# Pooling mixer as band matrices on TensorE, last norm's 1/sigma in PSUM, condition rows in the first MLP

## The chip, the cores and the metric

The kernel runs on one core of one Trainium2 chip, with five engines (PE multiplies matrices; DVE, ACT and POOL work on vectors; SP issues the DMAs), SBUF as working memory and PSUM as the place where PE's sums stand. The metric is the device time of one execution in microseconds, as the median over runs. A profiled execution also leaves a trace with a row for each instruction.

## The reference

One step of a four-layer backbone: 128 prompt tokens and 256 sample tokens, 1024 features, F32. Each layer has a mixer and a squared-ReLU MLP, each followed by a layer norm of ALPHA * x + g * out, with shift, scale and gate from a condition vector (one for the prompt, one for the sample). The mixers are an RG-LRU, a short convolution, multi-scale pooling and the RG-LRU again. The change concerns the third, which subtracts each token from the mean of a window around it (2, 4, 8 or 16 tokens, one window for each quarter of the features, clipped at the sequence's ends) and multiplies each quarter by its own 256 x 256 matrix:

```python
def pool_mixer(x, w, scale):
    ...
    for g, win in enumerate(POOL_WINDOWS):
        lo = jnp.clip(t - win // 2, 0, T)
        hi = jnp.clip(t + win - win // 2, 0, T)
        ...
        s = jnp.take(Sg, hi, axis=1) - jnp.take(Sg, lo, axis=1)
        pooled.append(s / cnt[None, :, None])
    d = (jnp.concatenate(pooled, axis=-1) - xf).astype(x.dtype)
    y = jnp.einsum('btgc,gcd->btgd', d.reshape(bsz, T, N_POOL_GROUPS, POOL_GROUP), w)
    return y.reshape(bsz, T, D_MODEL) * scale
```

and then the layer's last steps, `x = layer_norm(ALPHA * x + g1 * out, ...)` and the MLP with its own norm.

## The kernel before

**Tiles.** Activations lie feature-major: X is eight tiles of 128 features x 384 tokens (128 prompt, 256 sample). Weights stream from HBM in tiles of 1 MB ("raw", four buffers, loaded by SP at L1280), each sixteen blocks of 128 x 128. Half a tile at a time is split into a rounded part `whi` (ACT, L1292) and a rest `wlo` (DVE, L1298), three halves ahead of use. A product is three matmuls in the reduced-precision type fp32r, hi x hi, lo x hi and hi x lo (`mm3`, L195; rows L197, L198, L199), each moving 384 tokens through a stationary weight block. Sums over features, and the modulation's matrix-vector products, use matmuls in full F32.

**Order.** The program is a list of items, most of them a half tile of weights with its blocks. `tick` counts blocks, and `defer(n, f)` keeps f for n ticks later, so work of DVE, ACT and POOL is put between PE's blocks by numbers in the code. A scheduler then sets the row of each engine. Each engine works its row in order.

**A layer norm.** `ln_evac` (L553) takes each finished output tile: `resid` (L549) adds it into X on DVE, one instruction for the prompt's columns and one for the sample's. After tile 0, `shift` (L569, L570) makes `ssb`, its mean over features, and L572 subtracts it from every tile to keep sums small (POOL; DVE for some). L584 squares on ACT; POOL adds tiles into `s1t` (L599), and DVE or POOL squares into `s2t`. `ln_tail` (L611) multiplies `s1t`, `s2t` and the last tile by ones (L621 to L624), and then `tail` (L636) makes 1/sigma on DVE: variance (L650), first guess `y0` (ACT, L651), a Newton step (L655 to L657) into `r`; all these are SBUF tiles `tmp`. L641 subtracts the mean from X (in the last norm POOL does six tiles of it, L649), `chunk` (L660) multiplies a tile by `r` (L661), modulates it (L702, L707), and splits it into the hi and lo pieces of `h` (L720, L725) for the next product. While this runs PE has only modulation products (`gemv`, L347) that were parked for it.

**The pooling layer.** `pool_alloc` (on POOL) clears padded buffers. The tail in front, `ln_tail(4, ..., lazy=True)`, only makes `r`; six of its mean subtractions are on POOL. `pool_mix` (L1132) drives the rest from inside the matrix product: ahead of each group's first block, `stage` scales two tiles (L674), modulates them into padded buffers (L707), and `pool_stage` (L1101) makes window sums on DVE by additions or a scan (L1115 to L1121), corrects the edges (L1129), subtracts the token itself (L1130), and splits, hi on ACT (L720) and lo on POOL (L725). The product then moves 392 columns (L197 to L199). Here L590 adds each tile and its square into the statistics at once by F32 matmuls.

**Condition rows.** `setup_rows` (L424) loads two rows of 1024 conditions and makes silu of them by L427 (ACT), L428 and L429 (DVE), 2048 columns each. `mac` (L432) uses them on DVE (L450) for some modulation products, fed by SP's loads `fetch`.

**Ends.** In `tail`, the last norm's tiles go through `final_y` (L796; L801 on ACT) to the output.

## Time and profile before

| what | value |
|---|---|
| median of three runs | 1638.74 us (1637.17 to 1639.63) |
| the profiled execution's own time | 1636.94 us |
| its span, first to last instruction | 1635.2 us |
| mean granted TensorE clock | 0.987 |
| PE busy | 1568.7 us (96%) |
| DVE busy | 1169.3 us (72%) |
| ACT busy | 751.8 us (46%) |
| POOL busy | 400.6 us (24%) |
| HBM read | 285.64 MB, 176 GB/s over the span |

A busy PE is not PE at its peak: matmuls are pipelined, so a matmul recorded as 0.34 us can start 0.17 us behind the one before. A row of a timeline gives start, duration, engine, line and operation, output <- inputs, shape, the number of instructions in the row (x2), and in square brackets how long the engine was idle before it and which instruction released it. A row of groups gives the busy time and the mean in ns, then the idle time before its instructions and who ended it. In the rows of windows the numbers in brackets are instructions, and the last three columns are the granted clock (1.00 is full), the DMA engines' busy share and GB/s. "PEld" is PE's loading of stationary blocks.

### The profile page before, as it was taken

To read this page: it belongs to the slowest core of one execution; us is meant where nothing else is said; L and a number is where in the kernel's file an instruction comes from. 1 tells how busy PE (TensorE), PEld (TensorE's weight loads), DVE (VectorE), ACT (ScalarE), POOL (GpSimd) and SP (SyncE) were. 2 spreads that over 40 slices of the span, in tenths; PEclk is the share of its full clock that TensorE was granted. 3 is DMA by queue.
4 is the path that set the end of the run, shared out by engine and by line. 5 is a ranking of instruction groups with operands and counts; after the bars stand their busy time and mean duration, and the time that the engine had idled before them with its cause. 6 is when DMAs were issued, how large, how long until landed. Compare 5 with 4: busy or idle time off the path is not lost.

```text
span 1635.2 us, 23710 instructions
## 1 busy us (share of the span) xinstructions
PE 1568.7 (96%) x9304; PEld 1496.4 (92%) x9304; DVE 1169.3 (72%) x1791; ACT 751.8 (46%) x1131; POOL 400.6 (24%) x442
## 2 busy tenths in 40 slices
PE   7999899999999999999997899999999989999996
PEld 6778799999999999999995599999988779999995
DVE  4789999964475569985547899975468997434544
ACT  3796553243253346324434553244359946423432
POOL 2113280002320058110045270000441134000043
PEclk9999999999999999999998999999999999999998
DMA  9776457755343545763533256745333444333321
GB/s 356 271 277 240 181 209 254 269 191 186 126 157 128 184 152 183 257 258 129 196 136 129 105 195 253 272 157 203 129 113 107 158 144 152 128 121 115 126 78 39
DMA packets 42304, 288.77 MB, mean 177 GB/s; under 512 B 4816, under 2 KB 6992, under 8 KB 8144
## 3 DMA queue, kind: packets, MB, share of 16 engines
q1 hardware_dynamic: 42192, 287.25, 49.0%
q8 instruction: 73, 1.20, 0.3%
q14 instruction: 39, 0.32, 0.1%
HBM read 285.64 MB, written 1.59 MB: 176 GB/s over the span
## 4 chain that ended last, share of the span: by engine, by line
PE 79%; DVE 12%; ACT 5%; issue 2%; POOL 1%; DMA 1%; SPq 0%; DVEq 0%; POOLq 0%; ACTq 0%
PE acc L199 26%; PE acc L198 26%; PE acc L197 25%; DVE wlo L1298 2%; DVE lru L881 1%; ACT hidf L932 1%; DMA raw<-in_wmod 1%; DVE hidf L960 1%; DVE X L549 1%; DVE X L572 1%; ACT L935 1%; ACT hidf L935 1%; DVE X L661 1%; DVE hidf L949 1%; POOL h L725 1%
## 5 line engine op out<-in xcount | busy, mean ns | idle before, releaser
L1292 ACT ACTIVATE whi<-raw 128x1024 fp32r<-128x1024 f32 x338 | 356.2, 1056 | 420.2 <-PE acc L199 347.9
L1298 DVE TENSOR_TENSOR wlo<-raw,whi 128x1024 fp32r<-128x1024 f32 x338 | 436.3, 1292 | 156.3 <-ACT whi L1292 155.9
L197 PE MATMUL acc<-h,whi 128*128 128x384 f32 (+2 forms) x1488 | 507.3, 341 | 16.0 <-ACT h L720 10.5
L198 PE MATMUL acc<-h,wlo 128*128 128x384 f32 (+2 forms) x1488 | 505.3, 340 | 0.0
L199 PE MATMUL acc<-h,whi 128*128 128x384 f32 (+2 forms) x1488 | 476.8, 340 | 3.2 <-POOL h L725 3.2
L197 PE MATMUL acc<-hid,whi 128*128 128x384 f32 (+1 forms) x1216 | 411.4, 338 | 0.8 <-ACT hid L977 0.8
L199 PE MATMUL acc<-hid,whi 128*128 128x384 f32 (+1 forms) x1216 | 409.3, 337 | 0.9 <-DVE hid L981 0.9
L198 PE MATMUL acc<-hid,wlo 128*128 128x384 f32 (+1 forms) x1216 | 409.0, 336 | 0.0
L197 PEld LDWEIGHTS acc<-h,whi 128*128 128x128 f32 x1488 | 281.3, 189 | 24.7 <-ACT h L720 11.6
L199 PEld LDWEIGHTS acc<-h,whi 128*128 128x128 f32 x1488 | 278.3, 189 | 6.7 <-POOL h L725 5.0
L198 PEld LDWEIGHTS acc<-h,wlo 128*128 128x128 f32 x1488 | 281.1, 189 | 1.6 <-issue 0.5
L197 PEld LDWEIGHTS acc<-hid,whi 128*128 128x128 f32 x1216 | 228.3, 188 | 2.4 <-ACT hid L977 1.5
L199 PEld LDWEIGHTS acc<-hid,whi 128*128 128x128 f32 x1216 | 228.3, 188 | 1.5 <-DVE hid L981 1.5
L198 PEld LDWEIGHTS acc<-hid,wlo 128*128 128x128 f32 x1216 | 228.3, 188 | 0.9
L450 DVE SCALAR_TENSOR_TENSOR mac<-mac,silb 128x1024 f32<-128x1024 f32 x176 | 216.1, 1228 | 1.7
L832 ACT ACTIVATE tmp<-acc,par 128x384 f32<-128x384 f32 x128 | 74.2, 580 | 248.1 <-PE acc L199 248.1
L572 POOL TENSOR_TENSOR X<-X,ssb 128x384 f32<-128x384 f32 x49 | 56.1, 1179 | 488.7 <-ACT ssb L570 488.7
L834 DVE TENSOR_TENSOR tmp<-tmp 128x384 f32<-128x384 f32 x128 | 73.3, 572 | 104.2 <-ACT tmp L832 104.2
L549 DVE SCALAR_TENSOR_TENSOR X<-acc,m,X 128x128 f32<-128x128 f32 (+1 forms) x176 | 64.7, 411 | 113.9 <-PE acc L199 112.0
L779 POOL TENSOR_SCALAR X<-X,ag,xbb 128x128 f32<-128x128 f32 x64 | 126.9, 1997 | 0.4
L416 POOL TENSOR_SCALAR sc<-m 128x16 f32<-128x16 f32 x7 | 6.4, 911 | 270.8 <-DVE m L464 269.4
L835 DVE TENSOR_TENSOR hid<-tmp,hid 128x384 fp32r<-128x384 f32 x128 | 72.3, 565 | 0.3
(192 smaller groups left out, 1207.1 us busy)
## 6 DMA issues: line engine op xcount, KB each, us to landing
raw<-in_w SPq DMA_DIRECT2D x128, 1024.0 KB, 4.9
mac<-in_wmodv SPq DMA_DIRECT2D x44, 1024.0 KB, 5.0
raw<-in_wmodp SPq DMA_DIRECT2D x26, 1024.0 KB, 4.9
park<-in_wmodp SPq DMA_DIRECT2D x18, 1024.0 KB, 8.4
raw<-in_lin SPq DMA_DIRECT2D x16, 1024.0 KB, 5.1
raw<-in_scin SPq DMA_DIRECT2D x12, 1024.0 KB, 4.9
raw<-in_wmod SPq DMA_DIRECT2D x8, 1024.0 KB, 7.8
raw<-in_lout SPq DMA_DIRECT2D x8, 1024.0 KB, 5.0
```

The costliest lines, as they stand in the source:

```text
L197: pe.matmul(ps, lhsT=hi, rhs=xhi, start=first, stop=False)
L198: pe.matmul(ps, lhsT=lo, rhs=xhi, start=False, stop=False)
L199: late = lambda: pe.matmul(ps, lhsT=hi, rhs=xlo, start=False, stop=last)
L450: vec.scalar_tensor_tensor(prod, raw[i % 2][:, D * q : D * q + D], 1.0, silb[:, D * k : D * k + D], op0=ALU.mult, op1=ALU.mult, accum_out= ...
L549: vec.scalar_tensor_tensor(Xt[c][:, o : o + n], ps[:, a:b], col(g, c, k), Xt[c][:, o : o + n], op0=ALU.mult, op1=ALU.add)
L572: (vec if fast and i > 2 else gp).tensor_tensor(Xt[i], Xt[i], ssb, op=ALU.subtract)
L779: gp.tensor_scalar(Xt[c][:, a:b], Xt[c][:, a:b], col(g, c, k), col(xb, c, k), op0=ALU.mult, op1=ALU.add)
L832: act.activation(r, ps[:, :T], AF.Relu, bias=par_t[:, i : i + 1])
L834: vec.tensor_tensor(q, r, r, op=ALU.mult)
L835: vec.tensor_tensor(lo, q, hi.bitcast(F32), op=ALU.subtract)
L1292: act.activation(hi, raws[id(raw)][:, i * 1024 : (i + 1) * 1024], AF.Copy)
L1298: vec.tensor_tensor(lo, raws[id(raw)][:, i * 1024 : (i + 1) * 1024], hi.bitcast(F32), op=ALU.subtract)
```

## The change

**Pooling.** A window mean minus the token itself is linear in the tokens, so it can be multiplied by a matrix over tokens that is zero outside a band along its diagonal. The new `pool_mix` first multiplies by the weights and then by the band. First stage: for each 128-token block t and group g, z = h^T W, with the block of h stationary and 256 columns of weights moving, three matmuls per k as in `mm3`; two groups share a PSUM buffer of 512 columns, and six such buffers arise. Each is split into hi and lo (ACT L237, DVE L238) in buffers of the MLP's `hid`. Second stage, `second`: for each output tile nine matmuls (L1149) with z stationary and pieces of the band moving, 128, 128, 128, 256, 8, 136, 136, 8 and 136 columns (1064 in all). `first` calls it for tile 0 behind the chunk of X5, for tile 1 behind X6, for the rest behind X7. The tail in front, `ln_tail(4)`, is now an ordinary one with eight chunks. In `ln_evac` for this layer the shift of every tile is on DVE (L571, L581), POOL adds s1t, and the squares are kept and summed by F32 matmuls at the statistics.

**The bands.** `band_load` fetches 128 x 1040 of the bands twice through the raw buffers, copies each into a rounded constant (ACT, L1091) and makes the rest of the parts that need it (DVE, L1095). Both stand behind `ln_tail(2)` in the program.

**Last norm.** For idx 8 the tiles `y0` and `r` are taken from PSUM.

**Condition rows.** `setup_rows` is called from the first `mac` with one of its weight buffers as scratch; its three steps are deferred by 6, 10 and 14 ticks and the second fetch by 15.

In ACT's row around ln_tail(2), `acc` is a PSUM buffer, `tmp_4225` and `tmp_4226` the first chunk. Before, its square of X7 (X_103) is followed by the variance's square, by y0 (L651) and the chunks:

```order
L584 ACTIVATE tmp_4097<-X_102 128x384
L584 ACTIVATE tmp_4158<-X_103 128x384
L643 ACTIVATE tmp_4211<-acc_4160 128x384
L651 ACTIVATE tmp_4213<-tmp_4212 128x384
L707 ACTIVATE tmp_4225<-X_96,bb_2962,gg_2961 128x128
```

After, at the same place, with y0 now L653:

```order
L592 ACTIVATE tmp_4098<-X_102 128x384
L1091 ACTIVATE band<-raw_4119 128x1040
L592 ACTIVATE tmp_4159<-X_103 128x384
L645 ACTIVATE tmp_4212<-acc_4161 128x384
L1091 ACTIVATE band<-raw_4200 128x1040
L653 ACTIVATE tmp_4215<-tmp_4213 128x384
L703 ACTIVATE tmp_4226<-X_96,bb_2963,gg_2962 128x128
```

The two copies stand ahead of the square of X7 and ahead of y0; nothing else has moved here.

DVE's row there after the change, where L657 to L659 are the Newton step:

```order
L657 TENSOR_TENSOR tmp_4214<-tmp_4213,tmp_4215 128x384
L1095 TENSOR_TENSOR fine<-raw_4200,band 128x2x128
L658 SCALAR_TENSOR_TENSOR tmp_4214<-tmp_4214,tmp_4215 128x384
L1095 TENSOR_TENSOR fine<-raw_4200,band 128x2x8 x2
L659 SCALAR_TENSOR_TENSOR tmp_4216<-tmp_4214,tmp_4215 128x384
```

The second band's pieces stand between the Newton step's instructions; the first band's stand ahead of X7's residual.

DVE's row in the pooling layer (X_96 is X0 and so on; `hidf` are the padded buffers). Before, behind tile 2's residual:

```order
L572 TENSOR_TENSOR X_99<-X_99,ssb 128x384
L572 TENSOR_TENSOR X_100<-X_100,ssb 128x384
L572 TENSOR_TENSOR X_101<-X_101,ssb 128x384
L1121 SCALAR_TENSOR_TENSOR hidf_7855<-hidf_7854,hidf_7880 128x408
L1121 SCALAR_TENSOR_TENSOR hidf_7856<-hidf_7854,hidf_7884 128x408
L1124 TENSOR_TENSOR hidf_7857<-hidf_7855 128x392
L1124 TENSOR_TENSOR hidf_7858<-hidf_7856 128x392
L549 SCALAR_TENSOR_TENSOR X_99<-acc_8094,g_7976,X_99 128x128
L549 SCALAR_TENSOR_TENSOR X_99<-acc_8094,g_7976,X_99 128x256
```

After, from the fourth z split on:

```order
L556 SCALAR_TENSOR_TENSOR X_97<-acc_8115,g_8003,X_97 128x256
L238 TENSOR_TENSOR z_8151<-acc_8077,z_8150 128x512
L238 TENSOR_TENSOR z_8155<-acc_8081,z_8154 128x512
L581 TENSOR_TENSOR X_96<-X_96,ssb 128x384
L581 TENSOR_TENSOR X_97<-X_97,ssb 128x384
L556 SCALAR_TENSOR_TENSOR X_98<-acc_8158,g_8003,X_98 128x128
L556 SCALAR_TENSOR_TENSOR X_98<-acc_8158,g_8003,X_98 128x256
L571 TENSOR_TENSOR X_98<-X_98,ssb 128x384
L556 SCALAR_TENSOR_TENSOR X_99<-acc_8174,g_8003,X_99 128x128
```

The window sums between the residuals are gone, and each residual is followed by its own shift.

The scaling of the condition rows in DVE's row, before and then after; `mac` and `sb` are its scratch:

```order
L1298 TENSOR_TENSOR wlo_1519<-raw_1310,whi_1518 128x1024
L549 SCALAR_TENSOR_TENSOR X_96<-acc_1383,m_854,X_96 128x128
L549 SCALAR_TENSOR_TENSOR X_96<-acc_1383,m_854,X_96 128x256
L428 TENSOR_SCALAR sb_1844<-sb_1844 128x2048
L1298 TENSOR_TENSOR wlo_1563<-raw_1310,whi_1562 128x1024
```

```order
L1293 TENSOR_TENSOR wlo_1521<-raw_1312,whi_1520 128x1024
L556 SCALAR_TENSOR_TENSOR X_96<-acc_1385,m_856,X_96 128x128
L556 SCALAR_TENSOR_TENSOR X_96<-acc_1385,m_856,X_96 128x256
L430 TENSOR_SCALAR mac_1845<-mac_1845 128x2048
L1293 TENSOR_TENSOR wlo_1565<-raw_1312,whi_1564 128x1024
```

It keeps its place; so do the Tanh on ACT and the multiply on DVE.

The diff, cut to its core:

```diff
-    def setup_rows(crow):
+    rows_ready = []
+
+    def setup_rows(t):
         nc.sync.dma_start(silb, crow)
-        t = scr.tile([P, NSCR], F32, tag="scr", name=nm("sb"))[:, : 2 * D]
-        act.activation(t, silb, AF.Tanh, scale=0.5)
-        vec.tensor_scalar(t, t, 1.0, 0.5, op0=ALU.add, op1=ALU.mult)
-        vec.tensor_tensor(silb, t, silb, op=ALU.mult)
+        defer(6, lambda: act.activation(t, silb, AF.Tanh, scale=0.5))
+        defer(10, lambda: vec.tensor_scalar(t, t, 1.0, 0.5, op0=ALU.add, op1=ALU.mult))
+        defer(14, lambda: vec.tensor_tensor(silb, t, silb, op=ALU.mult))
+        rows_ready.append(True)
...
         fetch(0)
-        fetch(1)
+        if rows_ready:
+            fetch(1)
+        else:
+            setup_rows(raw[1])
+            defer(15, lambda: fetch(1))
...
             elif 0 in sq:
+                if late:
+                    vec.tensor_tensor(Xt[c], Xt[c], ssb, op=ALU.subtract)
                 stat(c)
...
-            for i in range(6 if late else C):
-                (vec if fast and i > 2 else gp).tensor_tensor(Xt[i], Xt[i], ssb, op=ALU.subtract)
+            for i in [0] + held if late else range(C):
+                (vec if late or fast and i > 2 else gp).tensor_tensor(Xt[i], Xt[i], ssb, op=ALU.subtract)
             if late:
-                hcur["late"] = True
-                hcur["m"] = acc(), acc()
+                hcur["late"] = []
...
-                lag = hcur.get("lag")
-
-                def sums():
-                    for m, x in zip(hcur["m"], (Xt[c], sq[c])):
-                        pe.matmul(m[:, :T], lhsT=ones_m, rhs=x, start=(c == 0), stop=(c == C - 1))
-
-                hcur["lag"] = sums
-                if lag:
-                    lag()
-            elif c == 1:
-                gp.tensor_tensor(s1t, Xt[0], Xt[1], op=ALU.add)
-                s2eng.tensor_tensor(s2t, sq[0], sq[1], op=ALU.add)
-            elif 1 < c < 7:
-                gp.tensor_tensor(s1t, s1t, Xt[c], op=ALU.add)
-                s2eng.tensor_tensor(s2t, s2t, sq[c], op=ALU.add)
+                hcur["late"].append(sq[c])
+            if 0 < c < 7:
+                gp.tensor_tensor(s1t, Xt[0] if c == 1 else s1t, Xt[c], op=ALU.add)
+                if not late:
+                    s2eng.tensor_tensor(s2t, sq[0] if c == 1 else s2t, sq[c], op=ALU.add)
             elif c == 7:
                 hcur["sq7"] = sq[7]
...
+            many = hcur.pop("late", None)
+            if many:
+                for i, x in enumerate(many[:-1]):
+                    pe.matmul(m2[:, :T], lhsT=ones_m, rhs=x, start=i == 0, stop=False)
             pe.matmul(m1[:, :T], lhsT=ones_m, rhs=s1t, start=True, stop=False)
...
-            msq, v, y0, w, r = tmp(), tmp(), tmp(), tmp(), tmp()
+            last = idx == 2 * DEPTH
+            msq, v, w = tmp(), tmp(), tmp()
+            y0, r = (acc()[:, :T] if last else tmp() for _ in range(2))
...
-            on_pool = 2 if lazy or idx == 2 * DEPTH else C
+            on_pool = 2 if idx == 2 * DEPTH else C
...
-    def pool_alloc():
...
-    def pool_stage(c):
-        g = c // 2
-        win = WINDOWS[g]
-        b = pool_buf[c]
-        s, cs = pool_t["s"][c % 4], pool_t["cs"][c % 2]
-        o = 8 - win // 2
-        if win == 2:
-            vec.tensor_tensor(s[:, :PG], b[:, o : o + PG], b[:, o + 1 : o + 1 + PG], op=ALU.add)
-        elif win == 4:
-            n = PBUF - 1
-            vec.tensor_tensor(cs[:, 1 : 1 + n], b[:, :n], b[:, 1 : 1 + n], op=ALU.add)
-            vec.tensor_tensor(s[:, :PG], cs[:, 1 + o : 1 + o + PG], cs[:, 3 + o : 3 + o + PG], op=ALU.add)
-        else:
-            vec.tensor_tensor_scan(
-                cs[:, 1 : 1 + PBUF], pool_t["one"][:, :PBUF], b, 0.0, op0=ALU.mult, op1=ALU.add
-            )
-            vec.tensor_tensor(s[:, :PG], cs[:, o + win : o + win + PG], cs[:, o : o + PG], op=ALU.subtract)
-        e0 = PCOLS["pedge"][0] + 16 * g
-        edge = par_t[:, e0 : e0 + 16].rearrange("p (a b) -> p a b", b=8)
-        for at, step in ((0, TP - 8), (TP + 8, TS - 8)):
-            v = s[:, at : at + 2 * step].rearrange("p (a b) -> p a b", b=step)[:, :, 0:8]
-            vec.tensor_tensor(v, v, edge, op=ALU.mult)
-        vec.scalar_tensor_tensor(
-            s[:, :PG], s[:, :PG], 1.0 / win, b[:, 8 : 8 + PG], op0=ALU.mult, op1=ALU.subtract
-        )
-        new_h(c, s[:, :PG], PG, lo_eng=gp)()
...
+    def band_load(i):
+        n = 2 * NBAND
+
+        def f(raw):
+            two = lambda t, w: t.rearrange("p (g w) -> p g w", w=w)
+            src = two(raw[:, :n], NBAND)
+            hi = two(bandt[:, i * n : (i + 1) * n], NBAND)
+            lo = two(finet[:, i * 2 * NFINE : (i + 1) * 2 * NFINE], NFINE)
+            act.activation(hi, src, AF.Copy)
+            o = 0
+            for a, w in ((0, P), (BAND[0], HALO), (NBAND - HALO, HALO)):
+                x = slice(a, a + w)
+                vec.tensor_tensor(lo[:, :, o : o + w], src[:, :, x], hi[:, :, x].bitcast(F32), op=ALU.subtract)
+                o += w
+
+        G(band[i], f)
...
     def pool_mix(l):
+        zps, z = {}, {}
+        done = ln_evac(2 * l, segs=((TS, T, 0), (0, TS, TP)), fast=True, late=True)
+
+        def first(g, k):
+            def f(hi, lo):
+                p, o = g // 2, g % 2 * 256
+                for t in range(3):
+                    if g % 2 == 0 and k == 0:
+                        zps[p, t] = acc()
+                    ps = zps[p, t][:, o : o + 256]
+                    xhi, xlo = (x[:, t * P : (t + 1) * P] for x in hcur[2 * g + k])
+                    pe.matmul(ps, lhsT=xhi, rhs=hi, start=k == 0, stop=False)
+                    pe.matmul(ps, lhsT=xhi, rhs=lo, start=False, stop=False)
+                    pe.matmul(ps, lhsT=xlo, rhs=hi, start=False, stop=k == 1)
+                if g % 2 == 1 and k == 1:
+                    for t in range(3):
+                        hi_, lo_ = (hidp.tile([P, 2 * LB], F32R, tag="hid", name=nm("z"))[:, :512] for _ in range(2))
+                        split_hi_lo(zps[p, t], hi_, lo_)
+                        z[p, t] = (hi_, lo_)
+                if g >= 2:
+                    for c in {(2, 1): (0,), (3, 0): (1,), (3, 1): range(2, C)}.get((g, k), ()):
+                        second(c)
+                        tick()
+
+            return f
+
+        def second(c):
+            g = c // 2
+            ps = acc()
+            f0 = c % 4 * P
+            w = lambda t, i: z[g // 2, t][i][:, f0 : f0 + P]
+            m = lambda i: bandt[:, g * NBAND + sum(BAND[:i]) : g * NBAND + sum(BAND[: i + 1])]
+            fine = finet[:, g * NFINE : (g + 1) * NFINE]
+            y, yp = ps[:, :TS], ps[:, TS:T]
+            left, right = y[:, : P + HALO], y[:, P - HALO :]
+            for n, (o, t, i, x) in enumerate(
+                (
+                    (yp, 0, 0, m(0)),
+                    (yp, 0, 0, fine[:, :P]),
+                    (yp, 0, 1, m(0)),
+                    (y, 1, 0, m(1)),
+                    (y[:, :HALO], 1, 0, fine[:, P : P + HALO]),
+                    (left, 1, 1, m(1)[:, : P + HALO]),
+                    (right, 2, 0, m(2)),
+                    (y[:, TS - HALO :], 2, 0, fine[:, P + HALO :]),
+                    (right, 2, 1, m(2)),
+                )
+            ):
+                pe.matmul(o, lhsT=w(t, i), rhs=x, start=n in (0, 3), stop=n in (2, 8))
+            done(c, ps)
+
+        raw = ["raw", poolw, 2]
+        for i in range(2):
+            items.append(("w", raw, i, [first(2 * i + g, k) for g in range(2) for k in range(2)]))
...
-    X(lambda: setup_rows(crow))
     use = mlp(0, ORD_MOD_DVE[0])
     ln_tail(2, to_h(2, "mm"), use)
+    band_load(0)
+    band_load(1)
     use = short_conv(1)
     ln_tail(3, to_h(3, "mm"), use)
     use = mlp(1, ORD_MOD_DVE[1])
-    X(pool_alloc)
-    ln_tail(4, to_h(4, "pool"), use, lazy=True)
+    ln_tail(4, to_h(4, "mm"), use)
     pool_mix(2)
     ln_tail(5, to_h(5, "mm"), ng=4)
```

More of the change, by code (lines that the diff above doesn't have):

```diff
@@ L72 @@
 ORD_OUT = mouter(range(8), K8)
-ORD_POOL = [(2 * g + k, 2 * g + m) for g in range(4) for m in range(2) for k in range(2)]
+ORD_POOL = [(2 * g + k, 2 * g + m) for g in range(4) for k in range(2) for m in range(2)]
+HALO = 8
+BAND = (P, TS, P + HALO)
+NBAND = sum(BAND)
+NFINE = P + 2 * HALO
 SH1, SC1, G1, SH2, SC2, G2 = range(6)
@@ L116 @@
     ("psc", C * 2),
-    ("pedge", 64),
 ):
@@ L671, in chunk @@
                     hcur["end"] = nxt()
-            def scaled(c):
-                vec.tensor_tensor(Xt[c], Xt[c], r, op=ALU.mult)
-                return dst(c)
-            hcur["scaled"] = scaled
             hcur["first"] = []
             with tc.issue_after(done_r.ins):
-                if not lazy:
-                    chunk(0)
-                    with ExitStack() as es:
-                        for ins in hcur["first"]:
-                            es.enter_context(tc.issue_after(ins.ins))
-                        chunk(1)
-                    for c in range(2, C):
-                        chunk(c)
-                        if c == MARK + 1:
-                            late_splits()
+                chunk(0)
+                with ExitStack() as es:
+                    for ins in hcur["first"]:
+                        es.enter_context(tc.issue_after(ins.ins))
+                    chunk(1)
+                for c in range(2, C):
+                    chunk(c)
+                    if c == MARK + 1:
+                        late_splits()
                 late_splits()
@@ new lines, in backbone_kernel @@
+    finet = const.tile([P, 4 * NFINE], F32R, tag="fine", name="fine")
+    def band_load(i):
[12 more added lines that the diff above has]
+        G(band[i], f)
```

107 lines of the change are left out of this document (32 added, 75 removed).

## Prediction

> **What bounds the kernel now.** I read the page first: the span, and the chain of work that ended last.
>
> ```profile
> span 1635.2 us, 23710 instructions
> PE 79%; DVE 12%; ACT 5%; issue 2%; POOL 1%; DMA 1%; SPq 0%; DVEq 0%; POOLq 0%; ACTq 0%
> ```
>
> Four fifths of the chain are matmuls. The change leaves those of the MLPs and of the other mixers alone, so it can win only in the stretches where the chain runs on DVE and ACT, which are the layer norms and the pooling layer. Next I cut the run into windows: one of ordinary matrix work (the header gives the columns), then three inside the pooling layer.
>
> ```profile
> core 0: us, PE busy (x) PEld busy (x) DVE busy (x) ACT busy (x) POOL busy (x), PEclk, DMA share, GB/s
> 140.00:150.00 10.00, 10.00 (x58) 10.00 (x58) 9.58 (x14) 5.46 (x7) 3.65 (x10) 1.00 0.83 329
> ```
> ```profile
> 881.00:891.00 10.00, 0.05 (x4) 0.00 (x0) 10.00 (x21) 5.87 (x13) 4.37 (x5) 0.73 0.70 238
> 891.00:899.00 8.00, 5.79 (x16) 4.77 (x17) 7.75 (x16) 5.00 (x10) 5.64 (x4) 0.50 0.24 99
> 899.00:911.00 12.00, 8.54 (x27) 5.03 (x26) 12.00 (x20) 6.59 (x13) 7.56 (x7) 0.93 0.01 1
> ```
>
> In ordinary work PE takes 58 matmuls in 10 us, 0.172 us each. In the pooling layer it stands still from 881 to 891, runs at a granted clock of 0.50 until 899, and DVE is full from 881 to 911: DVE bounds this layer. The chain and the timelines of DVE and PE give its ends. L650 is the first step of 1/sigma in each tail, so from the L650 of ln_tail(4) to that of ln_tail(5) runs exactly the layer that the change replaces.
>
> ```profile
> 874.02 0.65 PE acc L621 x2
> 876.74 0.56 DVE tmp L650
> ```
> ```profile
> 891.02 0.69 PE L197 MATMUL acc<-h,whi 128*128 128x392 f32 x1 [9.97 <-ACT h L720]
> 894.23 0.69 PE L199 MATMUL acc<-h,whi 128*128 128x392 f32 x1 [2.19 <-POOL h L725]
> ```
> ```profile
> 923.89 0.56 DVE L650 SCALAR_TENSOR_TENSOR tmp<-acc,tmp 128x384 f32<-128x384 f32 x1 [1.88 <-PE acc L590]
> 927.07 0.56 DVE L661 TENSOR_TENSOR X<-X,tmp 128x384 f32<-128x384 f32 x1
> ```
>
> It takes 923.89 - 876.74 = 47.15 us, and its first matmul starts 14.3 us after L650. In the tail of ln_tail(5), which is of the ordinary kind, the first chunk's multiply comes 3.18 us after L650. A full-precision statistics matmul of 384 columns (two records in a row of the chain) takes 0.65 us.
>
> **Term 1, the pooling layer: -9.3 us.** The change removes the window sums, the edges, POOL's lo pieces and the lazy tail; it adds an ordinary tail, a first stage per chunk, six z splits, and narrow matmuls. I take the new layer in five steps, with rows of the ordinary tail ln_tail(2) on DVE and four groups.
>
> ```profile
> 460.10 0.56 DVE L661 TENSOR_TENSOR X<-X,tmp 128x384 f32<-128x384 f32 x1
> 476.53 0.57 DVE L725 TENSOR_TENSOR h<-tmp,h 128x384 fp32r<-128x384 f32 x1
> ```
> ```profile
> L572 DVE TENSOR_TENSOR X<-X,ssb 128x384 f32<-128x384 f32 x13 | 13.0, 1061 | 0.5 <-ACT ssb L570 0.5
> L549 DVE SCALAR_TENSOR_TENSOR X<-acc,g,X 128x128 f32<-128x128 f32 (+1 forms) x16 | 5.9, 412 | 3.2 <-PE acc L199 3.0
> L599 POOL TENSOR_TENSOR s1t<-s1t,X 128x384 f32<-128x384 f32 x35 | 38.6, 1103 | 105.9 <-DVE X L549 105.5
> L641 DVE TENSOR_TENSOR X<-X,acc 128x384 f32<-128x384 f32 x52 | 27.3, 547 | 0.0
> ```
>
> (a) The first chunk's multiply at 876.74 + 3.18 = 879.9. (b) From the first multiply to the last lo, ln_tail(2) takes 476.53 + 0.57 - 460.10 = 17.0 us for its eight chunks with the weight splits between them; the new tail has fewer weight splits and one z split there, so I take the same: last lo at 896.9. Behind it PE owes nine matmuls of 256 columns; by columns they cost 0.172 x 256/384 = 0.115 us each, 1.03 us per chunk against a chunk pace of 17.0/8 = 2.1, so PE keeps up and ends at 897.3 (some of the nine need only the hi piece). (c) DVE then does five z splits, two residuals and two shifts. A split has 512 columns and one operand in PSUM, as L641: 0.547 x 512/384 = 0.73, taken as 0.7. A residual has two parts, 0.37 each as in the row of X7 quoted under term 3. That is 5 x 0.7 + 2 x 0.74 + 2 x 0.55 = 6.1: 903.0. (d) Six tiles follow, each with a residual, a shift on DVE and an addition on POOL. L572 takes 1.06 us, about twice the 0.55 of L641: it is the one with both inputs in SBUF, and POOL's L599 runs beside it. So I let shift and addition take turns, 0.55 + 1.10 = 1.65 per tile, with the residual beside the addition: X7 is shifted at 903.0 + 9.9 = 912.9. (e) POOL's sum over X6 ends at 912.9 - 1.65 + 1.10 = 912.4; three statistics matmuls of 0.65 follow, and L650 comes 0.13 behind the last as at 876.74 (four sums from 874.02 end at 876.62): 914.5 to 914.6 against 923.89. The earlier squares' matmuls (seven in PSUM instead of additions) fall into PE's idle time between tiles. Gain 9.3.
>
> Bounds of this term. If shift and addition do not hold each other up, DVE's 1.29 per tile paces (d) and 6 x 0.36 = 2.2 more is won: 11.5. The unknown is the narrow matmul: none below 384 columns with both operands split stands in the trace. Lower price: the columns at 0.172/384 = 0.45 ns, or the weight load's pitch if that is longer; two loads start 0.10 us apart here:
>
> ```profile
> 928.51 0.19 PEld L197 LDWEIGHTS acc<-h,whi 128*128 128x128 f32 x1 [2.48 <-issue]
> 928.61 0.19 PEld L198 LDWEIGHTS acc<-h,wlo 128*128 128x128 f32 x1
> ```
>
> That is at most 9 x 0.10 = 0.9 us per output tile, below the 1.65 of (d). Upper price: that of the statistics matmul, 0.65/384 = 1.69 ns a column, so 1064 columns x 1.69 = 1.8 us per tile; what it does is rival A. I take the lower one, since the row of the same operand type is the nearest. The Trainium skill ("FP8 and Floating Point Precision", section TensorE Precision Notes) says that reduced-precision FP32 is read truncated in one pass and true FP32 takes four, with no word on narrow ones; the two prices here stand 3.8 to 1, which agrees at 384 columns, and by that rule rival A would not occur.
>
> What is late next: weights. In 899 to 911 the DMA engines moved nothing (share 0.01), so the next halves have long landed, and the layer behind can start 9.3 earlier.
>
> **Term 2, the last layer norm: -2.7 us.** Nothing follows it, so all of it is on the chain.
>
> ```profile
> 1620.28 7.02 POOL L649 TENSOR_TENSOR X<-X,tmp 128x384 f32<-128x384 f32 x6 [8.29 <-ACT tmp L647]
> ```
> ```profile
> 1620.56 1.01 DVE L641 TENSOR_TENSOR X<-X,acc 128x384 f32<-128x384 f32 x2
> 1621.49 1.17 DVE L655 TENSOR_TENSOR tmp<-tmp,tmp 128x384 f32<-128x384 f32 x1
> 1622.68 1.23 DVE L656 SCALAR_TENSOR_TENSOR tmp<-tmp,tmp 128x384 f32<-128x384 f32 x1
> 1624.02 1.16 DVE L657 SCALAR_TENSOR_TENSOR tmp<-tmp,tmp 128x384 f32<-128x384 f32 x1
> 1625.22 3.44 DVE L661 TENSOR_TENSOR X<-X,tmp 128x384 f32<-128x384 f32 x4
> ```
>
> Beside POOL's six subtractions L641, which reads PSUM, takes 0.5 each, while L655 to L657, with both inputs in SBUF, take 1.16 to 1.23. With y0 and r in PSUM each of these has an operand there: 3 x 0.62 = 1.9 saved. The multiplies L661 get r from PSUM too; the four take 3.44 instead of 4 x 0.56 = 2.24, so 1.2 more. Of these 3.1 up to 1.0 can be lost where DVE reaches a tile before POOL's subtraction of it is done (six take 7.02, 1.17 each): I take 2.7, with 2.2 and 3.2 as ends.
>
> **Term 3, the band loads: +2.0 us.** They stand where scin's first load stood, behind the first MLP.
>
> ```profile
> 448.90 0.33 SPq L1280 DMA_DIRECT2D raw<-in_scin  x1
> ```
> ```profile
> raw<-in_scin SPq DMA_DIRECT2D x12, 1024.0 KB, 4.9
> ```
> ```profile
> raw<-in_lgate SPq DMA_DIRECT2D x8, 512.0 KB, 3.6
> ```
> ```profile
> L1292 ACT ACTIVATE whi<-raw 128x1024 fp32r<-128x1024 f32 x338 | 356.2, 1056 | 420.2 <-PE acc L199 347.9 <-issue 70.2 <-DVE wlo L1298 1.3
> ```
> ```profile
> 454.24 0.74 DVE L549 SCALAR_TENSOR_TENSOR X<-acc,m,X 128x128 f32<-128x128 f32 x2 [5.36 <-PE acc L199]
> ```
> ```profile
> 457.45 0.53 ACT L651 ACTIVATE tmp<-tmp 128x384 f32<-128x384 f32 x1 [0.85 <-DVE tmp L650]
> ```
> ```profile
> 470.28 1.05 ACT L1292 ACTIVATE whi<-raw 128x1024 fp32r<-128x1024 f32 x1
> ```
> ```profile
> 460.00:462.00 2.00, 1.60 (x27) 0.90 (x20) 1.87 (x6) 1.01 (x3) 0.16 (x1) 1.00 0.27 57
> ```
>
> The first band load, issued at 448.90, lands after 3.6 us at 452.5; ACT copies 1040 columns in 1.08 (L1292) until 453.6, and DVE's fine pieces (272 columns, some 0.55 by L641 with three starts) end by 454.2, inside DVE's idle 5.36 ahead of X7's residual. The second load gets its buffer only then: 454.2 + 3.6 = 457.8, copy until 458.9. That copy stands ahead of y0 (L651, L653 of after) in ACT's row, so y0 ends at 459.4 instead of 457.98: +1.45. Its fine pieces stand between the Newton steps on DVE: +0.55. Queued behind are the rest of 1/sigma and the eight chunks, and PE waits for them: in 460 to 462 it has 0.4 us idle, with modulation matmuls as its only cover. So +2.0 goes through; if the second load found a buffer early only the 0.5 on DVE would remain, and if it came with the longer latency of other loads +3. On SP's queue scin's third tile, which took this place before, now follows both bands through the same buffer: issued at about 461.5 and landed by 466.5 with the 4.9 that the page's DMA part gives such a load, ahead of its split at 470.28. That costs nothing.
>
> **Term 4, the set-up rows: 0.** Tanh, the scaling and the multiply by the row are the same instructions, now spread over ticks, and each stands at the same place in its engine's row as before (shown with the change).
>
> ```profile
> 152.11 1.92 ACT L427 ACTIVATE sb<-silb 128x2048 f32<-128x2048 f32 x1 [1.14 <-DVE hid L981]
> ```
> ```profile
> 154.06 1.23 DVE L428 TENSOR_SCALAR sb<-sb 128x2048 f32<-128x2048 f32 x1 [0.25 <-ACT sb L427]
> 165.81 2.28 DVE L429 TENSOR_TENSOR silb<-sb,silb 128x2048 f32<-128x2048 f32 x1
> ```
> ```profile
> 175.85 1.65 PE L621 MATMUL acc<-s1t,ones_m 128*128 128x384 f32 x2 [5.13 <-POOL s1t L599]
> ```
>
> The cover they would need is not there: DVE is full here, and PE waits 5.13 us at 175.85. If they did leave this stretch up to 1.23 + 2.28 = 3.5 us would be won (rival D). The second modulation load is put off behind them; nothing waits for it then.
>
> **Sum.** -9.3 - 2.7 + 2.0 = -10.0 us. The profiled execution took 1636.94 us, 1.80 below the median of the runs (1638.74), so it becomes 1626.9 and the median 1628.7. The forecast's own ends are -11.5 - 3.2 + 0.5 = -14.2 and, with the narrow matmuls dear and the loads late, -7.8 - 2.2 + 3.0 = -7.0.
>
> **The rivals.**
>
> A. Matmuls below 256 columns run at the statistics rate. Two output tiles stand between the last chunks on PE: 1.03 + 1.8 = 2.83 against a pace of 2.1, so the last chunk's matmuls end 1.5 later; the other six cost PE 1.8 each but stay ahead of DVE. Term 1 falls to 7.8, the sum to -8.5: 1630.2. For it speaks that no such row exists; against it the operand type. Chance 0.25.
>
> B, the other side. The 256-column matmuls of the first stage run at that rate as well: 0.43 us each, 3.9 per chunk, 31.2 for eight from 881.4, plus 3.6 for the two output tiles: 916.2 instead of 897.3. Of the 17.3 us behind it some 3 can be done earlier, so L650 comes at about 930.5, +6.6; with -2.7 + 2.0 the kernel is slower by about 6 to 8: 1645.7. It decides from the point where the last chunk comes 10 us late: (897.3 + 10 - 881.4)/8 = 3.2 us per chunk, 0.36 per matmul. Chance 0.11.
>
> C. PE's clock is halved through the layer, as in 891 to 899 of before (0.50). The first stage is then 2.1 per chunk, at the pace; the two output tiles between cost some 2 more, the three last sums 3 x 0.65 = 2, and the earlier squares' sums up to 1: the gain falls to between 4.3 and 5.3, the sum to about -5.5: 1633.2. The Trainium skill ("TensorE: Matmul & The Clock Gate", Part 1) says that the clock falls to half after an idle window of about 3.4 us and returns after one of sustained work. The drop behind 10 us of idleness agrees; in the new layer PE would pause under 1.1 us between chunks, so by that rule C does not come. Since 899 to 911 still shows 0.93 with PE 71% busy, I leave it 0.10.
>
> D. The set-up rows do leave the full stretch: -13.5, 1625.2. The order speaks against it. Chance 0.04.
>
> E. The change doesn't bring what it says in the pooling layer: the chunks are as slow as the stages were, so that term 1 is nothing and the sum -0.7: 1638.0. Against it: before, POOL makes the lo pieces, and a matmul waits 2.19 us for one at 894.23; the new tail makes them on DVE. Chance 0.08.
>
> **How the numbers follow.** My forecast keeps 0.42. About 0.2%, 3.3 us, is what a measurement here tells from no change. Faster by more: the forecast, A, D and most of C (0.08), 0.79. Same: E and the rest of C, 0.10. Slower: B, 0.11. The range runs from the forecast's low end, 1624.5, to C with its terms at their dear ends (-4.3 - 2.2 + 3.0 = -3.5: 1635.2), each put 0.8 further out, half of the 1.57 by which a run shown lies from its median: 1623.7 to 1636.0. It leaves out B and E, 0.19.
>
> **What would show it.** L650 of the fifth norm (L652 in the new numbering) some 38 us behind that of the fourth instead of 47.15; first matmul of the layer about 5 us behind it instead of 14.3; 256-column matmuls at 0.115 us; a granted clock near 1; in the last norm the three Newton steps at 0.55; y0 of ln_tail(2) 1.4 us late behind a band copy. Wrong would be: PE busy throughout the pooling layer (A, B), a clock of 0.5 (C), or a second band load that lands before the first copy ends.

## The result, and the profile after

The changed kernel takes 1624.29 us (median of four runs, 1623.06 to 1628.32) against 1638.83 us: a ratio of 0.9917, 95% interval 0.9898 to 0.9936. It is faster by 14.5 us where 10.0 were forecast (1628.7, range 1623.7 to 1636.0). Four more runs of it in a later comparison gave 1625.80 us and 0.9926 (0.9909 to 0.9942), 13.4 us. The profiled execution took 1623.76 us.

The page of the changed kernel, with the span and the chain's shares:

```profile
span 1621.9 us, 23848 instructions
...
PE 79%; DVE 12%; ACT 5%; issue 2%; DMA 1%; POOL 1%; SPq 0%; DVEq 0%; POOLq 0%; ACTq 0%
```

The shares haven't moved; 13.3 us have gone out of the span. To see from where, I take the start of each norm's variance (L650 before, L652 after) and so cut the run into stretches, each an MLP or a mixer with the tail ahead of it. Their lengths in us:

| stretch | before | after | after, again |
|---|---|---|---|
| to norm 1 (first LRU layer) | 180.38 | 181.20 | 181.61 |
| to norm 2 (first MLP) | 276.48 | 276.49 | 276.48 |
| to norm 3 (short convolution; band loads) | 142.95 | 144.27 | 144.06 |
| to norm 4 (second MLP) | 276.93 | 276.93 | 276.91 |
| to norm 5 (pooling) | 47.15 | 35.52 | 35.55 |
| to norm 6 (third MLP) | 279.20 | 277.97 | 277.95 |
| to norm 7 (second LRU layer) | 140.60 | 140.58 | 140.60 |
| to norm 8 (last MLP) | 276.40 | 276.80 | 276.79 |
| to the end of the span | 15.11 | 12.14 | 12.15 |

The pooling layer gave 11.6, the last norm 3.0; the band loads took 1.3. The windows of the changed pooling layer (columns as in the prediction: PE, PEld, DVE, ACT, POOL, granted clock, DMA share, GB/s):

```profile
882.00:892.00 10.00, 7.41 (x63) 5.56 (x56) 9.87 (x21) 8.91 (x18) 4.24 (x5) 1.00 0.57 213
892.00:900.80 8.80, 7.76 (x54) 6.70 (x53) 8.57 (x19) 6.53 (x14) 4.03 (x5) 1.00 0.26 87
900.80:907.20 6.40, 6.40 (x57) 6.26 (x56) 6.30 (x14) 2.53 (x5) 2.90 (x3) 1.00 0.11 45
907.20:914.40 7.20, 6.99 (x25) 3.66 (x28) 5.09 (x10) 2.68 (x6) 3.10 (x4) 1.00 0.01 2
```

DVE is full until X7's shift ends at 912.4, as it was full before, but it has less to do: 32.8 us of work between the two L652, against 41.9 between the two L650. PE no longer stands still: from 900.8 on it is full too but for 0.2 us, at a granted clock of 1.00. The timeline of DVE behind the last chunk's lo piece (L721) shows the steps (c) and (d) of the prediction, and POOL's beside it:

```profile
897.73 1.88 DVE L238 TENSOR_TENSOR z<-acc,z 128x512 fp32r<-128x512 f32 x3
899.53 1.38 DVE L556 SCALAR_TENSOR_TENSOR X<-acc,g,X 128x128 f32<-128x128 f32 x4
900.83 1.28 DVE L238 TENSOR_TENSOR z<-acc,z 128x512 fp32r<-128x512 f32 x2
902.02 1.01 DVE L581 TENSOR_TENSOR X<-X,ssb 128x384 f32<-128x384 f32 x2
902.96 0.73 DVE L556 SCALAR_TENSOR_TENSOR X<-acc,g,X 128x128 f32<-128x128 f32 x2
903.73 0.88 DVE L571 TENSOR_TENSOR X<-X,ssb 128x384 f32<-128x384 f32 x1
904.53 0.73 DVE L556 SCALAR_TENSOR_TENSOR X<-acc,g,X 128x128 f32<-128x128 f32 x2
...
911.52 0.87 DVE L571 TENSOR_TENSOR X<-X,ssb 128x384 f32<-128x384 f32 x1
```
```profile
903.18 1.00 POOL L596 TENSOR_TENSOR s1t<-X,X 128x384 f32<-128x384 f32 x1 [5.30 <-DVE X L581]
904.75 1.00 POOL L596 TENSOR_TENSOR s1t<-s1t,X 128x384 f32<-128x384 f32 x1 [0.56 <-DVE X L571]
```

A tile takes 1.57 (902.96 to 904.53). Its shift L571 takes 0.88, while L581, with POOL idle, took 1.01 for two. The timeline of PE in the same place, with a part of one output tile's nine narrow matmuls and then the statistics (a sum in full F32 is two records):

```profile
901.58 0.17 PE L1149 MATMUL acc<-fine,z 128*128 128x8 f32 x1
901.61 0.42 PE L1149 MATMUL acc<-band,z 128*128 128x136 f32 x2
901.87 0.22 PE L1149 MATMUL acc<-fine,z 128*128 128x8 f32 x1
...
907.15 4.08 PE L619 MATMUL acc<-tmp,ones_m 128*128 128x384 f32 x12
911.45 0.91 PE L619 MATMUL acc<-tmp,ones_m 128*128 128x384 f32 x2 [0.21 <-ACT tmp L592]
912.19 0.81 PE L620 MATMUL acc<-s1t,ones_m 128*128 128x384 f32 x2
912.84 0.81 PE L623 MATMUL acc<-X,ones_m 128*128 128x384 f32 x2
913.48 0.81 PE L624 MATMUL acc<-tmp,ones_m 128*128 128x384 f32 x2
```

The seven squares' sums do not lie between the tiles: PE works its row in order, the sums stand behind all output tiles, and they run from 907.15 almost without a pause to the end. Only the seventh waits, 0.21 us, for the square behind DVE's shift of X6; three more sums follow it. The last norm of the changed kernel, on DVE:

```profile
1611.16 0.55 DVE L657 TENSOR_TENSOR tmp<-tmp,acc 128x384 f32<-128x384 f32 x1
1611.74 0.55 DVE L658 SCALAR_TENSOR_TENSOR tmp<-tmp,acc 128x384 f32<-128x384 f32 x1
1612.32 0.56 DVE L659 SCALAR_TENSOR_TENSOR acc<-tmp,acc 128x384 f32<-128x384 f32 x1
1612.92 1.95 DVE L663 TENSOR_TENSOR X<-X,acc 128x384 f32<-128x384 f32 x4
```

And the third norm, on ACT and on DVE:

```profile
458.60 1.07 ACT L1091 ACTIVATE band<-raw 128x1040 fp32r<-128x1040 f32 x1 [1.17 <-DMA raw<-in_band]
459.58 0.51 ACT L653 ACTIVATE tmp<-tmp 128x384 f32<-128x384 f32 x1
```
```profile
460.19 0.56 DVE L657 TENSOR_TENSOR tmp<-tmp,tmp 128x384 f32<-128x384 f32 x1 [1.01 <-ACT tmp L653]
460.66 0.42 DVE L1095 TENSOR_TENSOR fine<-raw,band 128x256 fp32r<-128x256 f32 x1
461.00 0.55 DVE L658 SCALAR_TENSOR_TENSOR tmp<-tmp,tmp 128x384 f32<-128x384 f32 x1
```

The second copy waits for its load and y0 (L653) stands behind it; DVE then waits 1.01 for y0.

### The profile page after: what moved, and what is told of

It is laid out like the page before. It is cut to its first block, busy times and chain, and to the rows that moved or that the text cites. A ratio compares the mean times of both kernels' runs of the same rounds, so it can differ in the third digit from the quotient of the medians.

```text
span 1621.9 us, 23848 instructions
## 1 busy us (share of the span) xinstructions
PE 1569.9 (97%) x9388; PEld 1500.4 (93%) x9388; DVE 1158.7 (71%) x1786; ACT 750.6 (46%) x1129; POOL 392.8 (24%) x410
## 4 chain that ended last, share of the span: by engine, by line
PE 79%; DVE 12%; ACT 5%; issue 2%; DMA 1%; POOL 1%; SPq 0%; DVEq 0%; POOLq 0%; ACTq 0%
PE acc L199 25%; PE acc L198 25%; PE acc L200 25%; DVE wlo L1293 2%; DVE lru L868 1%; ACT hidf L919 1%; DMA raw<-in_wmod 1%; DVE X L556 1%; DVE hidf L947 1%; DVE hidf L936 1%; ACT L922 1%; ACT hidf L922 1%; DVE X L663 1%; DVE X L581 0%; ACT L932 0%
## 5 line engine op out<-in xcount | busy, mean ns | idle before, releaser
L198 PE MATMUL acc<-h,whi 128*128 128x384 f32 (+2 forms) x1472 | 499.0, 339 | 7.2 <-DVE h L698 6.7
L199 PE MATMUL acc<-h,wlo 128*128 128x384 f32 (+2 forms) x1472 | 498.3, 339 | 0.0
L200 PE MATMUL acc<-h,whi 128*128 128x384 f32 (+2 forms) x1472 | 468.8, 339 | 0.0
L198 PEld LDWEIGHTS acc<-h,whi 128*128 128x128 f32 x1472 | 277.1, 188 | 14.7 <-issue 10.0
L199 PEld LDWEIGHTS acc<-h,wlo 128*128 128x128 f32 x1472 | 277.0, 188 | 1.0 <-issue 0.2
L200 PEld LDWEIGHTS acc<-h,whi 128*128 128x128 f32 x1472 | 273.7, 188 | 1.0 <-DVE X L643 0.4
L581 POOL TENSOR_TENSOR X<-X,ssb 128x384 f32<-128x384 f32 x46 | 52.5, 1178 | 488.1 <-ACT ssb L579 488.1
L771 POOL TENSOR_SCALAR X<-X,ag,xbb 128x128 f32<-128x128 f32 x64 | 134.2, 2112 | 0.4
L596 POOL TENSOR_TENSOR s1t<-s1t,X 128x384 f32<-128x384 f32 x40 | 43.7, 1092 | 114.4 <-DVE X L556 111.1
```

The source lines that it names most:

```text
L198: pe.matmul(ps, lhsT=hi, rhs=xhi, start=first, stop=False)
L199: pe.matmul(ps, lhsT=lo, rhs=xhi, start=False, stop=False)
L200: late = lambda: pe.matmul(ps, lhsT=hi, rhs=xlo, start=False, stop=last)
L581: (vec if late or fast and i > 2 else gp).tensor_tensor(Xt[i], Xt[i], ssb, op=ALU.subtract)
L771: gp.tensor_scalar(Xt[c][:, a:b], Xt[c][:, a:b], col(g, c, k), col(xb, c, k), op0=ALU.mult, op1=ALU.add)
```

## The experiments

Theory: three places carry the change, and each has the mechanism that the prediction gave it. For each edit the rival is that the stretch changed for another reason. The stretches named below are those of the table.

**e1, the last norm's y0 and r back in SBUF.**

```diff
-            y0, r = (acc()[:, :T] if last else tmp() for _ in range(2))
+            y0, r = tmp(), tmp()
```

> The changed kernel with y0 and r of the last norm back in SBUF. Theory (both inputs in SBUF make DVE slow beside POOL): from the last L652 to the end of the span 15.1 us instead of 12.1, the three Newton instructions at 1.15 to 1.25 us instead of 0.55, the multiplies beside POOL at 0.8 to 0.9; time +3.0, about 1627. Rival (the last stretch was shorter for another reason, such as where the rows stand): Newton instructions stay below 0.8 and the stretch grows by under 1 us.

Measured: 1628.81 us; the last stretch 14.97, every other one but the first (183.55, with later start-up loads) within 0.05 of the changed kernel. On DVE:

```profile
1613.53 1.16 DVE L657 TENSOR_TENSOR tmp<-tmp,tmp 128x384 f32<-128x384 f32 x1
...
1617.26 3.44 DVE L663 TENSOR_TENSOR X<-X,tmp 128x384 f32<-128x384 f32 x4
```

Both durations are those of before. The theory holds: 2.8 us.

**e2, the band loads in the second half of the second MLP.**

```diff
-    band_load(0)
-    band_load(1)
     use = short_conv(1)
     ln_tail(3, to_h(3, "mm"), use)
+    at = len(items)
     use = mlp(1, ORD_MOD_DVE[1])
+    for i, n in ((1, 56), (0, 42)):
+        band_load(i)
+        items.insert(at + n, items.pop())
```

> The changed kernel with the two band loads moved into the second half of the second MLP. Theory (the second copy ahead of y0 and the fine pieces between the Newton steps cost 1.3 us in the third norm): from L652 of the second norm to that of the third 143.0 us instead of 144.3, the second MLP as long as before (276.9 from norm to norm), the pooling layer unchanged at 35.5; time -1.3, about 1623. Rival (the loads cost as much anywhere, as they hold a weight buffer and stand in ACT's and DVE's rows): the second MLP grows by 1 us or more and the time stays at 1624.

Measured: the stretch to norm 3 falls to 142.94, that of before; the second MLP keeps its 276.93 and the pooling layer its 35.52. y0 now follows the variance at once:

```profile
458.92 0.52 ACT L653 ACTIVATE tmp<-tmp 128x384 f32<-128x384 f32 x1 [0.85 <-DVE tmp L652]
```

So the 1.3 us were the place, not the loads. The time, 1624.56 us, is not below that of the changed kernel: in this trace the stretch to norm 7 took 142.14 instead of 140.58, of which more in the last section. A gain of 1.3 us is below what these runs can tell.

**e3, POOL's sums over the tiles put on PE.**

```diff
-            if 0 < c < 7:
+            if 0 < c < 7 and not late:
                 gp.tensor_tensor(s1t, ...)
...
                 for i, x in enumerate(many[:-1]):
+                    pe.matmul(m1[:, :T], lhsT=ones_m, rhs=Xt[i], start=i == 0, stop=False)
                     pe.matmul(m2[:, :T], lhsT=ones_m, rhs=x, start=i == 0, stop=False)
...
```

> The changed kernel in which POOL no longer adds up the tiles of the pooling layer; their sums go over TensorE as those of the squares do, seven matmuls more. Theory (DVE's shift with both inputs in SBUF is held up by POOL's addition): L571 starts the next residual 0.5 us behind its own start instead of 0.80, a tile takes 1.25 instead of 1.56, and L652 of the fifth norm comes 33.0 us behind that of the fourth instead of 35.5; time -2.5, about 1622. Rival (0.80 is what this shift takes by itself): tiles stay at 1.5 to 1.6, only the sum behind the last tile is shorter, 34.9; time -0.6.

Measured: 38.91 us, slower by 3.4, and 1628.67 us. The first half of the theory holds: the shift falls to 0.56 and a tile to 1.25.

```profile
904.61 0.56 DVE L571 TENSOR_TENSOR X<-X,ssb 128x384 f32<-128x384 f32 x1
905.08 0.74 DVE L556 SCALAR_TENSOR_TENSOR X<-acc,g,X 128x128 f32<-128x128 f32 x2
905.86 0.56 DVE L571 TENSOR_TENSOR X<-X,ssb 128x384 f32<-128x384 f32 x1
```

The second half fails, and so does the rival. On PE the sixteen sums follow the last output tile without a gap:

```profile
907.88 0.31 PE L1149 MATMUL acc<-band,z 128*128 128x136 f32 x1
908.02 0.86 PE L618 MATMUL acc<-X,ones_m 128*128 128x384 f32 x2
...
917.75 0.81 PE L624 MATMUL acc<-tmp,ones_m 128*128 128x384 f32 x2
```

From 908.0 they take 16 x 0.65 = 10.4, six sums or 3.9 us more than the ten of the changed kernel; the layer grew by 3.4, so DVE's faster tiles gave 0.5. I had counted on idle time of PE that isn't there, as in the prediction's step (e). From here the theory of this layer was: in its tail PE and DVE are both full, and end within half a microsecond of each other.

**e6, seven of the nine narrow matmuls issued twice**, to ask whether PE sets the end.

```diff
+                if n not in (0, 3):
+                    pe.matmul(o, lhsT=w(t, i), rhs=x, start=False, stop=False)
                 pe.matmul(o, lhsT=w(t, i), rhs=x, start=n in (0, 3), stop=n in (2, 8))
```

> The changed kernel with seven of the nine narrow matmuls of each output tile issued twice (its pooling result is therefore not the reference's). Theory (from the first output tile on, TensorE is full until the statistics and sets the end of the layer): seven more at 0.10 to 0.11 us make 0.75 per tile, so from L652 of the fourth norm to that of the fifth 35.5 plus 4.5 for six tiles plus up to 1.0 for the two between the chunks, 40.0 to 41.0 us. Rival (DVE's residuals and shifts pace the tail and TensorE runs ahead of them, as the recorded reasoning had it): 35.5 to 36.8.

Measured: 40.96, as the theory had it. A tile takes 1.80 us on PE (1.01 in the changed kernel); DVE now waits for the last two tiles, and 5.24 us at the end:

```profile
911.81 0.74 DVE L556 SCALAR_TENSOR_TENSOR X<-acc,g,X 128x128 f32<-128x128 f32 x2 [0.28 <-PE acc L1151]
...
913.61 0.74 DVE L556 SCALAR_TENSOR_TENSOR X<-acc,g,X 128x128 f32<-128x128 f32 x2 [0.46 <-PE acc L1151]
...
920.18 0.56 DVE L652 SCALAR_TENSOR_TENSOR tmp<-acc,tmp 128x384 f32<-128x384 f32 x1 [5.24 <-PE acc L624]
```

**e9, e11 and e12: relieve DVE, then PE, then both.** e9 leaves out POOL's sums and with them the statistics matmul over s1t, e11 leaves out the three matmuls with fine pieces, e12 does both.

```diff
-                gp.tensor_tensor(s1t, Xt[0] if c == 1 else s1t, Xt[c], op=ALU.add)
                 if not late:
+                    gp.tensor_tensor(s1t, Xt[0] if c == 1 else s1t, Xt[c], op=ALU.add)
...
-            pe.matmul(m1[:, :T], lhsT=ones_m, rhs=s1t, start=True, stop=False)
             if not many:
+                pe.matmul(m1[:, :T], lhsT=ones_m, rhs=s1t, start=True, stop=False)
...
-                pe.matmul(o, lhsT=w(t, i), rhs=x, start=n in (0, 3), stop=n in (2, 8))
+                if n not in (1, 4, 7):
+                    pe.matmul(o, lhsT=w(t, i), rhs=x, start=n in (0, 3), stop=n in (2, 8))
```

> The changed kernel without POOL's sums over the tiles in the pooling layer, which are left out altogether, so that this norm's mean is taken over the last tile alone. Theory (TensorE and DVE end this layer within half a us of each other): DVE's tiles fall to 1.25 us as in the run with the sums on TensorE, the last shift comes 1.9 us earlier, but nine statistics matmuls of 0.65 stand behind the output tiles on TensorE: 34.5 us from norm to norm, 1.0 less than 35.5. Rival (DVE and POOL alone set the end): 33.3 us.

> The changed kernel without the three matmuls of each output tile that take the bands' fine pieces (left out, so the pooling result is rounded at the sequences' ends). Theory (TensorE and DVE are both full in the tail): output tiles at 0.67 us instead of 1.0 on TensorE, 2 us less there, but DVE's last shift stays 33.5 us behind L652 and two sums and the square follow, so 34.9 to 35.1 instead of 35.5. Rival (TensorE alone sets the end): 33.5.

> The changed kernel without the fine pieces' matmuls and without POOL's sums over the tiles (both left out, so the pooling result is rounded at the ends and the norm's mean is taken over the last tile). Theory (two full engines: only relieving both moves the end): 33.0 to 33.3 us from norm to norm, 2.4 less than 35.5, more than the two reliefs by themselves add up to (1.1 and 0.5). Rival (they are independent): 33.9.

Measured: 34.38, 35.51 and 32.94 us, against 35.52. In e9 DVE has time in hand and PE's sums run back to back behind the tiles:

```profile
908.59 4.73 PE L619 MATMUL acc<-tmp,ones_m 128*128 128x384 f32 x14
913.15 0.81 PE L623 MATMUL acc<-X,ones_m 128*128 128x384 f32 x2
```

In e11 it is the other way round; PE is early and the last three squares' sums each wait for their square, which waits for DVE's shift. Two of them:

```profile
911.06 0.91 PE L619 MATMUL acc<-tmp,ones_m 128*128 128x384 f32 x2 [0.41 <-ACT tmp L592]
912.62 0.91 PE L619 MATMUL acc<-tmp,ones_m 128*128 128x384 f32 x2 [0.64 <-ACT tmp L592]
```

The lengths fall by 1.1, by nothing (I had expected 0.5) and by 2.6. But e9 and e12 also have one sum of 0.65 less at the end of PE's row, so e9 is not a relief of DVE alone: taking 0.65 off each, DVE's relief wins 0.5, as in e3, PE's nothing, and both 1.9. Two full engines, then; DVE with POOL is the later one by a little.

**e7, the first stage three times**, at the point from which rival B was to decide.

```diff
-                    pe.matmul(ps, lhsT=xhi, rhs=hi, start=k == 0, stop=False)
...
+                    for n in range(3):
+                        pe.matmul(ps, lhsT=xhi, rhs=hi, start=k == 0 and n == 0, stop=False)
...
```

> The changed kernel with every matmul of the first stage issued three times (its pooling result is therefore not the reference's). That is 3.1 us of matmuls per chunk instead of 1.05, the point that the recorded reasoning gave for its slower case. Theory: the last chunk's matmuls end 10 us later and nothing behind them shortens, 45.5 to 46 us from norm to norm instead of 35.5, so the whole gain over 47.15 but 1 to 2 us is gone. Rival (the tail behind the last chunk shortens, since DVE's splits of the first half are done by then): 41 to 43 us.

Measured: 46.12, the theory's number, but in part by luck. A chunk's matmuls took 3.2 us, and the last of the first stage came 12.5 us later and not 10 (33.2 behind L652 instead of 20.7); the tail behind it was 1.9 shorter, which goes the rival's way, though not by splits: DVE had done the first two tiles' residuals and shifts ahead of it. At 3.2 us per chunk the pooling layer's gain is down to 1.0 us.

**e4, the set-up rows as before.**

```diff
+    X(lambda: setup_rows(crow))
     use = mlp(0, ORD_MOD_DVE[0])
...
-        if rows_ready:
-            fetch(1)
-        else:
-            setup_rows(raw[1])
-            defer(15, lambda: fetch(1))
+        fetch(1)
```

> The changed kernel with the set-up of the condition rows as it was before: own scratch, one piece, no deferred fetch. Theory (the three instructions stand at the same places in their rows either way): every stretch from norm to norm within 0.3 us but for the granted clock, the set-up instructions starting at the same times to 0.3 us, DVE equally full from 150 to 176; time within 0.2% of 1624.3. Rival (the change did take them off the path): the first norm 1 to 3.5 us later, time 1625 to 1628.

Measured: 1625.22 us, ratio to the kernel before 0.9921 (0.9906 to 0.9936), the same as with the change. The rows stand where they stood in both others:

```profile
152.25 1.92 ACT L428 ACTIVATE sb<-silb 128x2048 f32<-128x2048 f32 x1 [1.14 <-DVE hid L962]
154.21 1.23 DVE L429 TENSOR_SCALAR sb<-sb 128x2048 f32<-128x2048 f32 x1 [0.25 <-ACT sb L428]
```

The first norm came at 180.42, earlier than with the change, so the rival has nothing. The sums ahead of that norm start at 176.01 here, as in e10 (175.60 in the first trace of the changed kernel, 175.85 before); what differs behind that start is the clock (last section).

**e8, the kernel before with only y0 and r in PSUM.**

```diff
-            msq, v, y0, w, r = tmp(), tmp(), tmp(), tmp(), tmp()
+            msq, v, w = tmp(), tmp(), tmp()
+            y0, r = (acc()[:, :T] if idx == 2 * DEPTH else tmp() for _ in range(2))
```

> The kernel before with only y0 and r of the last norm in PSUM. Theory: the last stretch 12.1 us instead of 15.1, all other stretches as before, the pooling layer at 47.15 within 0.3; time -3.0, about 1635.5. Rival (part of the 47.15 was a low granted clock that comes and goes): the pooling layer differs by 1 us or more between this trace and that of before. Second rival (the gain needs the other changes): the last stretch stays above 14.

Measured: 1636.83 us, ratio 0.9987 (0.9978 to 0.9997). The pooling layer took 47.14, so that length belongs to the kernel before and not to a clock that comes and goes. The last stretch took 13.19, between theory and second rival. From the variance to the start of the last instruction on ACT it is 8.47, the 8.46 of the changed kernel and not the 11.25 of before; the rest is the end behind it, 4.72 here and 3.68 there. The computing part is the theory's 2.8; why the end behind it was longer in this trace stays open.

**e10, the changed kernel once more**, to tell chance from cause.

> The changed kernel itself once more, to tell chance from cause. Theory (the change moves only the third norm, the pooling layer and the last norm; what else differs between the traces is the start-up loads and the granted clock at the first norm, at the head of the third MLP and at the norm of the second LRU layer): 144.3, 35.5 and 12.1 to 13.2 us in the three stretches again, while the first norm lies anywhere from 180.2 to 183.6 and the third MLP is 278.0 or 279.5. Rival (the third MLP is shorter because of the change): 278.0 again and a first norm near 181.2.

Measured: the last column of the table at the top. The three changed stretches repeat within 0.03 but for the band loads' (0.21). So does the third MLP at 277.95, which was the rival's sign. But e11 and e4, with pooling layers of 35.5 as well, have 279.52 and 279.51, and e9, e12 and e6 279.5 to 279.6: the change does not fix it.

## Why the prediction was right, and where it was not

**The sum.** Forecast -9.3 - 2.7 + 2.0 + 0 = -10.0; in the span -11.6 - 3.0 + 1.3, which makes -13.3. The rest cancels by luck: +0.8 at norm 1, -1.2 in the third MLP (a difference of clock that the change does not fix, last section) and +0.4 in the last MLP. All three terms had the right sign and, but for step (e), the right mechanism; the first was 2.3 too small. It lies just past its low end of 11.5, yet not for the reason of that end, which was a shift and an addition that do not hold each other up: they did, and the surplus lies in steps (b), (c) and (d).

**Term 1.** Step (a) held: the first multiply came 3.24 behind L652. Step (b) was mis-sized: the eight chunks took 15.7 us, not 17.0, since only two weight splits fell among them; I had taken the ordinary tail's length whole, though I named the difference. Step (c) took 5.2 and not 6.1: a z split 0.63, two residuals 1.38, two shifts 1.01. Step (d) held, with its reason: 1.57 per tile for 1.65 (0.5 over six tiles), and 1.25 once POOL's addition was gone (e3, e9). Step (e) failed in its reason: "The earlier squares' matmuls (seven in PSUM instead of additions) fall into PE's idle time between tiles". There is none; the runs put a full PE in its place (e3, e6, e9). Its number was off by only 0.4 (2.0 from the end of X7's shift to L652, for 1.6 to 1.7), because PE and DVE end together; that is luck. PE busy throughout the layer had been named as a sign of rivals A and B; from 900.8 on it was there without either.

**The narrow matmul.** The lower price was right. A tile takes 1.01 (its piece of 128 fine columns starts at 901.19, 902.20 and so on to 906.25), nine matmuls at 0.11, where the columns alone would make 0.48: the price is that of one instruction with its weight load, the 0.10 of the quoted loads, and not of the columns. The Trainium skill ("FP8 and Floating Point Precision", TensorE Precision Notes) has reduced-precision FP32 read truncated and true FP32 in four passes. The trace agrees at 128 to 256 columns, where the statistics' 1.69 ns a column would make 0.22 to 0.43 us a matmul; at 8 columns the weight load would hide either price. So rivals A and B did not come. A's working was wrong all the same: it said that dear tiles would "stay ahead of DVE"; in e6 a tile took A's 1.8 us, and that cost 5.4 us, not 1.5. B's was near: at its turning point of 3.2 us per chunk 1.0 of the gain was left, with 1.9 us of the tail done earlier where it had some 3 (e7). C did not come: the granted clock was 1.00 throughout the layer, where PE's longest pause was 1.29 us, against 9.97 in before.

**Term 2** was -2.8 by e1, by the contention that was named: with an operand in PSUM the Newton step takes 0.55 beside POOL instead of 1.16 to 1.23.

**Term 3** was mis-sized, +1.3 for +2.0. y0 ended 2.40 behind the variance's start instead of 1.12, the 1.3 late that was forecast (1.45). But 0.2 of that was hidden: without the bands (e2) the Newton step starts only 1.40 behind the variance, since DVE's two L643 come first, and with them at 2.50. And the fine pieces stretched the way from L657 to the first multiply by 0.2 (2.05 against 1.84 in e2), not by 0.55. In the other traces with the bands in this place the stretch took 143.97 to 144.38, so +1.0 to +1.4, and 145.97 in e11, where the clock was low besides (last section).

**Term 4** was 0, by e4.

**Not foreseen:** the last MLP is 0.4 longer in every run of the changed kernel and its variants (276.77 to 276.81) than in before and e8 (276.40, 276.39). PE has no gap in it; what costs it is not settled.

## What to carry to other kernels

When work moves from a full vector engine to an idle matrix engine, write down the matrix engine's row in order to the stretch's end: its sums here stood behind everything that had been moved, and the idle time that was to hide them was gone. Two engines that end together hide each other, so relieve each alone and both together before saying which bounds. And an operand in PSUM is a cheap way out of contention between DVE and POOL where nothing else hides it, while a load's own copy and splits want a place where no 1/sigma stands behind them.
